# Where a softmax is divided by its sum: the weights, or the attention's output

## Chip, cores, metric

One of the eight cores of a Trainium2 chip. The time is the device time of one execution in microseconds; the median of the runs counts. Engines: TensorE (PE, with its weight loads PEld), VectorE (DVE), ScalarE (ACT), GpSimd (POOL), SyncE (SP, which issues loads).

## The reference

Two transformer blocks over 512 tokens of width 1024, in fp32. The parts that matter are the attentions of the two mixers; each block has one mixer.

```python
# first block, dsa_attention: 8 query heads of 64, one shared key/value head,
# of the keys up to the query's position the best 128 are kept
logits = einsum('bqhd,bqkd->bqhk', qb, k_sel) * attn_scale
p = softmax(where(valid, logits, -inf), axis=-1)
out = einsum('bqhk,bqkd->bqhd', p, v_sel)

# second block, blocked_attention, twice: 8 heads with keys of 64+32 and values of 64,
# and 8 query heads of 64 over 2 key/value heads
s = einsum("bqhgd,bkhd->bhgqk", qblk, k)
pr = softmax(s, axis=-1)
out = einsum("bhgqk,bkhd->bqhd", pr, v)
```

The first block also has a cross-attention to 256 memory tokens (4 heads of 256). Around them stand the feed-forward layers, gates, projections and norms.

## The kernel before

Activations lie feature-major, 128 features on the partitions and 512 tokens along the row, in eight tiles. Every large product is made of three matmuls over operands split into a high and a low part (`mm3`); VectorE makes the low parts and ScalarE the high ones, also for each weight that a load brings.

An attention is a series of units. A unit of the first mixer is one block of 128 queries with four heads (`group`, L878), 4 blocks x 2 groups = 8 units, with 128, 256, 384 or 512 keys. The second mixer has 8 units of one head with four query blocks each (`head`, L1323), then 8 units of `group` with 512 keys. Each unit first makes four logits tiles with queries on the partitions in three `lg` banks of PSUM and calls `softmax` (L826) on each: maximum over the row and the bias from it on VectorE (L833 or L836, L838 or L840), exponential on ScalarE, which also writes the row's sum into `z` (L841), reciprocal of `z` (L842) and multiplication of the 128 x n weights by it (L850). The tables `F4` and `F6` in `K` send one multiplication in four of `head` and of the first mixer to GpSimd; the rest is VectorE's.

Then `pv` (L864) goes over the key tiles: `turned` (L852) transposes the four weight tiles on TensorE into one of the two `tt` banks (L858), splits them (L860 on ScalarE, L861 on VectorE), and two matmuls add high and low part into the one `o` bank (L872, L873). The value operand holds the high part in columns 0 to 63 and the low part in 64 to 127, so the output stands in two halves of 64 partitions, which have to be added: ScalarE copies the lower half to SBUF (L875), and VectorE adds the upper one into the result (L893 in `group`, four pieces of 64 x 128; L1337 in `head`, one of 64 x 512). In the output the queries run along the row, so a factor for each query is a row there, while the sums are a column.

`overlapped` (L896) writes the program so: the logits and softmax of unit u + 1, then a piece of other work (gates, keys, queries: projections that give TensorE something to do), then `pv` of unit u. The order that the engines get is not that of the program: a planner goes through all instructions with the program's order as priority, with durations of its own, and puts each on its engine when its operands and a free buffer are there by its reckoning. Buffers of one tag are a ring: a bank is given away again when its last reader is done. On the chip each engine follows its list in order.

`row` (L588) was there before, for the norms: it transposes a column, broadcast to 128 x 128, so that each partition of a PSUM tile holds it as a row. In cross-attention (`cross`, L1131) 16 calls of `softmax` divide the weights too.

Of the kernel before, what the change touches and what calls it, by code (L numbers as in the profile page):

```python
# [14 lines left out]
AF = mybir.ActivationFunctionType  # L15
OP = mybir.AluOpType
# [3 lines left out]
P = 128  # L20
D = 1024
KD = D // P
S = 512
NT = S // P
M = 256
# [30 lines left out]
A, B = slice(0, S // 2), slice(S // 2, S)  # L56
# [3 lines left out]
K = {'slots': [32, 8, 5],  # L60
 'F1': 0,
 'F2': 0,
 'F3': 1,
 'F4': 'PVVV',
 'F5': 'VVVV',
 'F6': 'VVPV',
 'ga0': 4,
 'gb0': 4,
# [110 lines left out]
class Net:  # L179
# [643 lines left out]
        mm(ps[:, :n], lhsT=q[:, qs], rhs=hh[:, :n], start=True, stop=False)  # L823
        mm(ps[:, :n], lhsT=q[:, qs], rhs=ll[:, :n], start=False, stop=True)

    def softmax(self, ps, scale, n, bias=None, pool="V"):  # L826

        nc = self.nc
        p = self.tmp((P, n))
        m, nb, z = (self.small(t, [P, 1], 8) for t in ("sm_m", "sm_b", "sm_z"))  # L830
        src = ps[:, :n]
        if bias is not None:
            nc.vector.tensor_tensor_reduce(out=p, in0=src, in1=bias, op0=OP.add, op1=OP.max, scale=1.0, scalar=NEG, accum_out=m)  # L833
            src = p
        else:
            nc.vector.tensor_reduce(out=m, in_=src, axis=AX.X, op=OP.max)  # L836
        if isinstance(scale, float):
            nc.vector.tensor_scalar(nb, m, -scale, None, op0=OP.mult)  # L838
        else:
            nc.vector.scalar_tensor_tensor(nb, m, -1.0, scale, op0=OP.mult, op1=OP.mult)  # L840
        nc.scalar.activation(p, src, AF.Exp, bias=nb, scale=scale, accum_out=z)  # L841
        nc.vector.reciprocal(z, z)  # L842
        self.scale(p, p, z, pool)
        return p

    def scale(self, out, src, z, pool="V"):
        if pool == "A":
            self.nc.scalar.activation(out, src, AF.Copy, scale=z)
            return
        (self.nc.gpsimd if pool == "P" else self.nc.vector).tensor_scalar(out, src, z, None, op0=OP.mult)  # L850

    def turned(self, ps_, j):  # L852

# [7 lines left out]
        nc.vector.tensor_tensor(lo, ps[:, :n], hi.bitcast(F32), op=OP.subtract)  # L861
        return hi, lo

    def pv(self, ps_, v):  # L864


        mm = self.nc.tensor.matmul
        o = self.bank("o")
        last = len(v) - 1
        for j, vj in enumerate(v):  # L870
            hi, lo = self.turned(ps_, j)
            mm(o, lhsT=vj, rhs=hi, start=j == 0, stop=False)  # L872
            mm(o, lhsT=vj, rhs=lo, start=False, stop=j == last)  # L873
        low = self.slot("u", (64, S))
        self.nc.scalar.copy(low, o[64:128])  # L875
        return o, low

    def group(self, i, g, q, keys, v, ot, n, soft):  # L878

        nc = self.nc  # L880
        ps = []
        for j in range(4):
            hd = 4 * g + j
            l = self.bank("lg")

            self.logits(l, q[hd], hd % 2, i, keys, max(n, 2 * P))
            ps.append(soft(l, hd, j))
        yield
        o, low = self.pv(ps, v[: n // P])
        for e in range(2):  # L890
            for c in range(2):
                b = slice((2 * c + e) * P, (2 * c + e + 1) * P)
                nc.vector.tensor_tensor(  # L893
                    ot[2 * g + c][64 * e : 64 * e + 64, i * P : i * P + P], o[0:64, b], low[:, b], op=OP.add)

    def overlapped(self, units):  # L896

# [41 lines left out]
    def mix(self):  # L939
        self.phase = "mix"  # L940
        nc, h = self.nc, self.h
# [85 lines left out]
        def units():  # L1027
            for i in range(NT):
                for g in range(2):
                    yield self.group(i, g, qa, ka, v, ot, (i + 1) * P,  # L1030
                                     lambda l, hd, j: self.softmax(l, 0.125, (i + 1) * P, bias[i], pool=K["F6"][j])), [lambda: next(more_b, None)]

        self.overlapped(units())
        for _ in more_b:
# [96 lines left out]
    def cross(self):  # L1131
        self.phase = "cross"
        nc, h = self.nc, self.h
        xs, r, step = self.enter("xattn_pre_g")
        keys, vals, work = self.memory()
        self.begin([], step, work)
        self.attending = True
        os_ = []

        def head(hd):  # L1140
            q = [self.split(self.project("xattn_w_q", 2 * hd + d, xs, r), self.pair()) for d in range(2)]
            ps = []
            for i in range(NT):
                l = self.bank("lg")
                for d in range(2):
                    qq = tuple(part[:, i * P : i * P + P] for part in q[d])
                    self.mm3(l[:, :M], qq, keys[2 * hd + d], d == 0, d == 1)
                ps.append(self.softmax(l, 0.0625, M))
            yield
            pt = [self.turned(ps, j) for j in range(2)]  # L1150
            for d in range(2):
                o = self.bank("o" if d else "lg")
                c = (hd % 2) * M + d * P
                for j in range(2):
                    vv = tuple(part[:, c : c + P] for part in vals[hd // 2, j])
                    self.mm3(o, vv, pt[j], j == 0, j == 1)
                os_.append(self.split(o, self.pair()))

        self.overlapped((head(hd), ()) for hd in range(4))
        self.attending = False  # L1160
        f = [self.big(dt=F32) for _ in range(KD)]
        self.down("xattn_w_o", f, 0, os_, False, K["late:cross"])
        self.leave(f, "xattn_post_g")

    def mix2(self):
# [155 lines left out]
            next(more_a)  # L1321

        def head(hd, q, keys):  # L1323
            ps = []
            for i in range(NT):
                l = self.bank("lg")
                tok = slice(i * P, i * P + P)
                self.mm3(l, (q[0][:, tok], q[1][:, tok]), keys, True, True)
                ps.append(self.softmax(l, sca[:, i : i + 1], S, pool=K["F4"][i]))
            yield  # L1330
            o, low = self.pv(ps, [t[:, hd % 4, :] for t in va[hd // 4]])
            own = slice(64 * (hd % 2), 64 * (hd % 2) + 64)
            if K["oa"][hd] == "P":
                nc.scalar.copy(oa[hd // 2][own], o[0:64])
                nc.gpsimd.tensor_tensor(oa[hd // 2][own], oa[hd // 2][own], low, op=OP.add)
            else:
                nc.vector.tensor_tensor(oa[hd // 2][own], o[0:64], low, op=OP.add)  # L1337

        ob = []

        def units():
            for hd in range(H):
                yield head(hd, *ready[hd]), work.pop(0)
                if hd % 2 and hd + 1 < H:
                    ready.extend(prepare(hd + 1))
            for _ in more_a:
                pass
            ob.extend(self.big(dt=F32) for _ in range(4))
            for g in range(2):
                for i in range(NT):  # L1350
                    yield self.group(i, g, qb, kbs[g], vbs[g], ob, S,
                                     lambda l, hd, j: self.softmax(l, scb[hd // 2][:, 2 * i + hd % 2 : 2 * i + hd % 2 + 1], S, pool=K["F5"][j])), work.pop(0)

        self.overlapped(units())
        for _ in more_b:
# [278 lines left out]
```

## Time and profile before

| | us |
|---|---|
| median of 3 runs | 2098.67 |
| lowest, highest | 2090.48, 2103.62 |
| profiled execution, own time | 2091.38 |
| its span, first to last instruction | 2089.6 |

On a busy line a share belongs to the whole span; a window gives busy time in one stretch, so idle time of an engine there is the stretch less its figure. Matmuls overlap, and their ends are modelled, so a busy TensorE is not one at its peak. In the waits the engine left of the arrow stood idle until the one on the right was done.

### The profile page before, as it was taken

The page shows a single profiled execution, that of the slowest core. Times are in us where ns is not written, and L with a number is a line of the kernel's source. Part 1 is how long each engine was busy: PE and PEld are TensorE (multiplying, and loading weights), DVE is VectorE, ACT ScalarE, POOL GpSimd, SP SyncE. Part 2 cuts the span into 40 slices and gives each one's busy share as a digit, 9 for nine tenths or more (in the row PEclk, how much of TensorE's full clock was granted, in tenths as well). Part 3 has the DMA queues.
Part 4 walks back from the last instruction along what each step waited for, and adds up shares of the span by engine and source line. Part 5 has one row for each costly group of instructions (what it writes and reads, how often), then busy time and mean ns, then how long its engine had stood idle before and what let it go on. Part 6 is the DMA issues. An engine that isn't in the chain of part 4 may idle for free. (4 is left out here: it accounts for less than half of the span.)

```text
span 2089.6 us, 32337 instructions
## 1 busy us (share of the span) xinstructions
PE 2011.4 (96%) x12428; PEld 1766.1 (85%) x12428; DVE 1544.4 (74%) x2956; ACT 1101.7 (53%) x2052; POOL 254.4 (12%) x239
## 2 busy tenths in 40 slices
PE   8999999899999999999999998998999999999997
PEld 7899998778778888998999998776778888988997
DVE  7977786799775585587777869588987678666755
ACT  5644454673573454554445445467864436444752
POOL 2000002313331310040000003213100000000001
PEclk9999999899999999999999999999999999999999
DMA  5233333212222233221333342211112313323331
GB/s 163 91 112 97 106 107 122 71 61 91 91 71 95 77 120 103 93 70 51 113 110 102 106 141 72 66 41 51 41 41 81 114 31 122 99 89 104 112 101 41
DMA packets 66010, 186.43 MB, mean 89 GB/s; under 512 B 6976, under 2 KB 14144, under 8 KB 65856
## 3 DMA queue, kind: packets, MB, share of 16 engines
q1 hardware_dynamic: 63376, 180.97, 26.8%
q10 hardware_dynamic: 2448, 3.41, 0.5%
q8 instruction: 97, 1.59, 0.3%
q14 instruction: 57, 0.47, 0.1%
q0 software_dynamic: 32, 0.00, 0.0%
HBM read 182.25 MB, written 2.10 MB: 88 GB/s over the span
## 5 line engine op out<-in xcount | busy, mean ns | idle before, releaser
L290 PE MATMUL mm<-x,w 128*128 128x512 f32 (+1 forms) x2064 | 473.8, 379 | 0.0
L290 PE MATMUL mm<-b,w 128*128 128x256 f32 (+1 forms) x2625 | 448.6, 322 | 2.0 <-ACT b L510 1.8
L290 PEld LDWEIGHTS mm<-x,w 128*128 128x128 f32 x2064 | 364.0, 188 | 74.9 <-DVE v L1274 0.7
L290 PEld LDWEIGHTS mm<-b,w 128*128 128x128 f32 x2625 | 375.2, 188 | 48.9 <-ACT b L510 4.2
L252 ACT CAST w<-r 128x1024 fp32r<-128x1024 f32 (+2 forms) x256 | 229.8, 898 | 277.8 <-PE mm L290 118.0
L290 PE MATMUL lg<-x,w 128*128 128x256 f32 (+1 forms) x2460 | 348.6, 295 | 6.8 <-DVE t L1385 4.7
L253 DVE TENSOR_TENSOR w<-r,w 128x1024 fp32r<-128x1024 f32 (+2 forms) x254 | 267.8, 1055 | 116.3 <-ACT w L252 111.3
L290 PE MATMUL lg<-b,w 128*128 128x256 f32 (+1 forms) x1929 | 352.9, 334 | 0.0
L290 PEld LDWEIGHTS lg<-x,w 128*128 128x128 f32 x2460 | 315.9, 188 | 27.9 <-DVE t L1385 6.4
L290 PEld LDWEIGHTS lg<-b,w 128*128 128x128 f32 x1929 | 294.5, 188 | 42.1
L457 ACT CAST w<-r 128x1024 fp32r<-128x1024 f32 x147 | 154.6, 1053 | 138.1 <-PE lg L290 81.3
L458 DVE TENSOR_TENSOR w<-r,w 128x1024 fp32r<-128x1024 f32 x147 | 178.7, 1221 | 19.9 <-ACT w L457 19.4
L290 PE MATMUL mm<-x,u 128*128 128x256 f32 x756 | 108.1, 287 | 15.6 <-ACT x L513 7.1
L510 ACT CAST b<-t 128x512 fp32r<-128x512 f32 (+1 forms) x113 | 60.8, 539 | 112.5 <-DVE t L745 34.3
L290 PEld LDWEIGHTS mm<-x,u 128*128 128x128 f32 x756 | 96.9, 193 | 18.7 <-ACT x L513 7.5
L569 POOL TENSOR_TENSOR sh<-sh,sh 128x256 f32<-128x256 f32 x45 | 37.5, 834 | 502.8 <-ACT sh L563 499.9
L511 DVE TENSOR_TENSOR b<-t,b 128x512 fp32r<-128x512 f32 (+1 forms) x113 | 67.2, 596 | 26.3 <-ACT b L510 26.0
L569 POOL TENSOR_TENSOR sf<-sf,sf 128x256 f32<-128x256 f32 x28 | 23.3, 833 | 450.4 <-ACT sf L563 440.4
L563 ACT ACTIVATE sh<-h 128x256 f32<-128x256 f32 x128 | 49.9, 411 | 52.5 <-DVE h L630 22.7
L928 POOL TENSOR_TENSOR b<-b,rows 128x512 f32<-128x512 f32 x32 | 52.5, 1642 | 174.7 <-ACT b L926 174.7
L861 DVE TENSOR_TENSOR u<-tt,u 128x512 fp32r<-128x512 f32 x92 | 62.0, 684 | 9.9 <-ACT u L860 9.3
L290 PE MATMUL lg<-x,b 128*128 128x256 f32 x456 | 68.1, 291 | 0.0
(271 smaller groups left out, 2738.9 us busy)
## 6 DMA issues: line engine op xcount, KB each, us to landing
r<-in_ffn_w SPq DMA_DIRECT2D x86, 512.0 KB, 3.3
r<-in_w_in SPq DMA_DIRECT2D x64, 512.0 KB, 3.2
r<-in_ffn_w SPq DMA_DIRECT2D x68, 256.0 KB, 2.7
r<-in_w_up SPq DMA_DIRECT2D x32, 512.0 KB, 3.2
r<-in_w_down SPq DMA_DIRECT2D x32, 384.0 KB, 3.4
r<-in_ffn_w SPq DMA_DIRECT2D x16, 384.0 KB, 3.3
r<-in_w_out SPq DMA_DIRECT2D x8, 512.0 KB, 3.2
r<-in_xattn_w_k SPq DMA_DIRECT2D x8, 512.0 KB, 3.2
```

The source lines that it names most:

```text
L252: nc.scalar.copy(hi, raw)
L253: self.second.tensor_tensor(lo, raw, hi.bitcast(F32), op=OP.subtract)
L290: self.nc.tensor.matmul(ps, lhsT=lhsT, rhs=rhs, start=start, stop=stop, skip_group_check=on)
L457: nc.scalar.copy(hi, raw)
L458: nc.vector.tensor_tensor(lo, raw, hi.bitcast(F32), op=OP.subtract)
L510: nc.scalar.copy(hi, src)
L511: nc.vector.tensor_tensor(lo, src, hi.bitcast(F32), op=OP.subtract)
L563: nc.scalar.activation(t, x, AF.Square)
L569: eng.tensor_tensor(ts[0], ts[0], t, op=OP.add)
L861: nc.vector.tensor_tensor(lo, ps[:, :n], hi.bitcast(F32), op=OP.subtract)
L928: nc.gpsimd.tensor_tensor(t[:, tok], t[:, tok], r[:, tok], op=OP.mult)
```

## The change

`softmax` stops after the exponential and leaves its weights undivided; the sums of a unit's four tiles go into the four columns of one tile. `pv`, after the copy of the lower half, takes one reciprocal of the 128 x 4 sums, turns its four columns into a row of 512 factors with `row` (four transposes into a `tt` bank), and adds the two halves of the output into `low`. `group` and `head` then multiply `low` by the row of factors, in the pieces in which they added before. All these multiplications are VectorE's, and the tables that sent some work to GpSimd have no reader any more. Cross-attention keeps reciprocal and multiplication, written at its call.

```diff
--- before.py
+++ after.py
@@ -823,11 +823,12 @@
         mm(ps[:, :n], lhsT=q[:, qs], rhs=hh[:, :n], start=True, stop=False)
         mm(ps[:, :n], lhsT=q[:, qs], rhs=ll[:, :n], start=False, stop=True)
-    def softmax(self, ps, scale, n, bias=None, pool="V"):
+    def softmax(self, ps, scale, n, z, bias=None):
+
         nc = self.nc
         p = self.tmp((P, n))
-        m, nb, z = (self.small(t, [P, 1], 8) for t in ("sm_m", "sm_b", "sm_z"))
+        m, nb = (self.small(t, [P, 1], 8) for t in ("sm_m", "sm_b"))
         src = ps[:, :n]
         if bias is not None:
             nc.vector.tensor_tensor_reduce(out=p, in0=src, in1=bias, op0=OP.add, op1=OP.max, scale=1.0, scalar=NEG, accum_out=m)
@@ -839,15 +840,10 @@
         else:
             nc.vector.scalar_tensor_tensor(nb, m, -1.0, scale, op0=OP.mult, op1=OP.mult)
         nc.scalar.activation(p, src, AF.Exp, bias=nb, scale=scale, accum_out=z)
-        nc.vector.reciprocal(z, z)
-        self.scale(p, p, z, pool)
         return p
-    def scale(self, out, src, z, pool="V"):
-        if pool == "A":
-            self.nc.scalar.activation(out, src, AF.Copy, scale=z)
-            return
-        (self.nc.gpsimd if pool == "P" else self.nc.vector).tensor_scalar(out, src, z, None, op0=OP.mult)
+    def sums_of(self, count):
+        return self.small("sm_z", [P, count], 8)
     def turned(self, ps_, j):
@@ -861,7 +857,7 @@
         nc.vector.tensor_tensor(lo, ps[:, :n], hi.bitcast(F32), op=OP.subtract)
         return hi, lo
-    def pv(self, ps_, v):
+    def pv(self, ps_, z, v):
         mm = self.nc.tensor.matmul
@@ -873,25 +869,28 @@
             mm(o, lhsT=vj, rhs=lo, start=False, stop=j == last)
         low = self.slot("u", (64, S))
         self.nc.scalar.copy(low, o[64:128])
-        return o, low
+        self.nc.vector.reciprocal(z, z)
+        rz = self.row(z)
+        self.nc.vector.tensor_tensor(low, o[0:64], low, op=OP.add)
+        return low, rz[0:64]
     def group(self, i, g, q, keys, v, ot, n, soft):
         nc = self.nc
-        ps = []
+        ps, z = [], self.sums_of(4)
         for j in range(4):
             hd = 4 * g + j
             l = self.bank("lg")
             self.logits(l, q[hd], hd % 2, i, keys, max(n, 2 * P))
-            ps.append(soft(l, hd, j))
+            ps.append(soft(l, hd, z[:, j : j + 1]))
         yield
-        o, low = self.pv(ps, v[: n // P])
+        o, rz = self.pv(ps, z, v[: n // P])
         for e in range(2):
             for c in range(2):
                 b = slice((2 * c + e) * P, (2 * c + e + 1) * P)
                 nc.vector.tensor_tensor(
-                    ot[2 * g + c][64 * e : 64 * e + 64, i * P : i * P + P], o[0:64, b], low[:, b], op=OP.add)
+                    ot[2 * g + c][64 * e : 64 * e + 64, i * P : i * P + P], o[:, b], rz[:, b], op=OP.mult)
     def overlapped(self, units):
@@ -1028,7 +1027,7 @@
             for i in range(NT):
                 for g in range(2):
                     yield self.group(i, g, qa, ka, v, ot, (i + 1) * P,
-                                     lambda l, hd, j: self.softmax(l, 0.125, (i + 1) * P, bias[i], pool=K["F6"][j])), [lambda: next(more_b, None)]
+                                     lambda l, hd, z: self.softmax(l, 0.125, (i + 1) * P, z, bias[i])), [lambda: next(more_b, None)]
         self.overlapped(units())
         for _ in more_b:
@@ -1145,7 +1144,11 @@
                 for d in range(2):
                     qq = tuple(part[:, i * P : i * P + P] for part in q[d])
                     self.mm3(l[:, :M], qq, keys[2 * hd + d], d == 0, d == 1)
-                ps.append(self.softmax(l, 0.0625, M))
+                z = self.sums_of(1)
+                p = self.softmax(l, 0.0625, M, z)
+                nc.vector.reciprocal(z, z)
+                nc.vector.tensor_scalar(p, p, z, None, op0=OP.mult)
+                ps.append(p)
             yield
             pt = [self.turned(ps, j) for j in range(2)]
             for d in range(2):
@@ -1321,20 +1324,16 @@
             next(more_a)
         def head(hd, q, keys):
-            ps = []
+            ps, z = [], self.sums_of(NT)
             for i in range(NT):
                 l = self.bank("lg")
                 tok = slice(i * P, i * P + P)
                 self.mm3(l, (q[0][:, tok], q[1][:, tok]), keys, True, True)
-                ps.append(self.softmax(l, sca[:, i : i + 1], S, pool=K["F4"][i]))
+                ps.append(self.softmax(l, sca[:, i : i + 1], S, z[:, i : i + 1]))
             yield
-            o, low = self.pv(ps, [t[:, hd % 4, :] for t in va[hd // 4]])
+            o, rz = self.pv(ps, z, [t[:, hd % 4, :] for t in va[hd // 4]])
             own = slice(64 * (hd % 2), 64 * (hd % 2) + 64)
-            if K["oa"][hd] == "P":
-                nc.scalar.copy(oa[hd // 2][own], o[0:64])
-                nc.gpsimd.tensor_tensor(oa[hd // 2][own], oa[hd // 2][own], low, op=OP.add)
-            else:
-                nc.vector.tensor_tensor(oa[hd // 2][own], o[0:64], low, op=OP.add)
+            nc.vector.tensor_tensor(oa[hd // 2][own], o, rz, op=OP.mult)
         ob = []
@@ -1349,7 +1348,7 @@
             for g in range(2):
                 for i in range(NT):
                     yield self.group(i, g, qb, kbs[g], vbs[g], ob, S,
-                                     lambda l, hd, j: self.softmax(l, scb[hd // 2][:, 2 * i + hd % 2 : 2 * i + hd % 2 + 1], S, pool=K["F5"][j])), work.pop(0)
+                                     lambda l, hd, z: self.softmax(l, scb[hd // 2][:, 2 * i + hd % 2 : 2 * i + hd % 2 + 1], S, z)), work.pop(0)
         self.overlapped(units())
         for _ in more_b:
```

## Rows read from the trace of the kernel before

**Rows 1.** The page, busy times of the engines, and the granted clock in 40 slices:

```profile
PE 2011.4 (96%) x12428; PEld 1766.1 (85%) x12428; DVE 1544.4 (74%) x2956; ACT 1101.7 (53%) x2052; POOL 254.4 (12%) x239
...
PEclk9999999899999999999999999999999999999999
```

**Rows 2.** Windows over the three attentions of the mixers, with their columns:

```profile
core 0: us, PE busy (x) PEld busy (x) DVE busy (x) ACT busy (x) POOL busy (x), PEclk, DMA share, GB/s
546.00:606.00 60.00, 58.90 (x298) 47.59 (x297) 49.27 (x186) 44.89 (x106) 20.54 (x15) 1.00 0.16 53
1355.00:1470.00 115.00, 102.35 (x481) 78.19 (x480) 95.06 (x230) 84.33 (x166) 26.98 (x17) 0.97 0.13 45
1470.00:1580.00 110.00, 105.29 (x512) 80.26 (x511) 95.75 (x252) 80.16 (x154) 13.55 (x10) 1.00 0.13 44
```

**Rows 3.** Windows of 15 us inside the second mixer:

```profile
1400.00:1415.00 15.00, 13.61 (x69) 10.62 (x70) 14.60 (x34) 11.46 (x24) 1.57 (x1) 1.00 0.16 50
1415.00:1430.00 15.00, 10.54 (x52) 8.70 (x50) 10.25 (x28) 8.16 (x15) 2.01 (x2) 0.89 0.18 57
1430.00:1445.00 15.00, 11.62 (x50) 8.07 (x49) 12.49 (x26) 11.66 (x26) 7.14 (x5) 0.88 0.07 26
1445.00:1460.00 15.00, 15.00 (x75) 12.17 (x74) 14.38 (x35) 11.93 (x23) 3.89 (x2) 1.00 0.23 81
```

**Rows 4.** Chain, 1355-1470 and 1470-1580 by line; pieces (start, us, what) of 1355-1580:

```profile
by line: PE mm L290 27.8%; PE lg L290 14.8%; PE tt L858 6.6%; PE o L873 5.1%; DVE u L861 5.0%; PE o L872 4.1%; DVE t L850 3.8%; issue 3.4%; DVE sm_m L836 2.9%; DVE w L253 2.7%; ACT t L841 2.4%; DVE b L1255 2.3%; PE mm L1272 2.3%; DVE sm_b L
...
by line: PE mm L290 31.6%; PE o L872 8.6%; PE tt L858 8.6%; PE o L873 7.0%; PE lg L823 4.1%; issue 4.0%; PE lg L824 3.6%; ACT u L860 3.6%; POOL b L928 3.3%; DVE u L861 2.9%; DVE b L803 2.5%; ACT w L252 2.2%; DVE w L253 2.1%; DVE t L850 1.7%
...
1369.43 0.87 PE tt L858 x8
...
1414.34 5.61 PE mm L290 x24
```

**Rows 5.** Waits, 1355 to 1580 us: who <- for whom: us, times, longest:

```profile
ACT t L841 <- DVE sm_b L840: 12.5, 17, 1.6
PEld o L873 <- DVE u L861: 11.5, 14, 3.2
PEld o L872 <- ACT u L860: 10.1, 28, 1.5
...
PE mm L1293 <- DVE t L1290: 4.5, 1, 4.5
```

**Rows 6.** Windows of L850 alone (VectorE, GpSimd where any); line L842, ns min/median/max:

```profile
546.00:606.00 60.00, 10.78 (x24) 9.84 (x8) 1.00 0.16 53
1355.00:1470.00 115.00, 13.99 (x24) 13.66 (x8) 0.97 0.13 45
1470.00:1580.00 110.00, 16.36 (x32) 0.00 (x0) 1.00 0.13 44
...
L842 DVE RECIPROCAL sm_z<-sm_z x112: 136/156/166, 548.2 to 1567.1; 128x1 f32<-128x1 f32 x112
```

**Rows 7.** Lines by form: count, busy us, mean ns of one, idle before:

```profile
L893 DVE TENSOR_TENSOR b<-o,u 64x128 f32<-64x128 f32 x64 | 15.4, 278 | 5.2 <-ACT u L875 4.6
...
L875 ACT COPY u<-o 64x512 f32<-64x512 f32 x24 | 14.0, 584 | 14.1 <-PE o L873 13.6
...
L593 PE MATMUL tt<-ident,r 128*128 128x128 f32 x54 | 10.5, 281 | 5.5 <-DVE r L543 5.3
...
L1337 DVE TENSOR_TENSOR b<-o,u 64x512 f32<-64x512 f32 x8 | 5.5, 682 | 1.9 <-ACT u L875 1.6
```

**Rows 8.** Timeline, TensorE: last P·V matmul of a unit, next unit's transposes (first, last of 13):

```profile
576.88 0.48 PE L873 MATMUL o<-u,v 128*128 128x512 f32 x1
...
577.20 0.71 PE L858 MATMUL tt<-ident,t 128*128 128x128 f32 x5
...
1572.00 0.40 PE L873 MATMUL o<-u,v 128*128 128x512 f32 x1
1572.23 0.60 PE L858 MATMUL tt<-ident,t 128*128 128x128 f32 x4
```

## The prediction, made before the changed kernel was run

> **What bounds the kernel now.** I read the page's busy times first, then windows over the stretches that the change touches, then the chain of work and the waits inside them. On the page TensorE is busy for 96% of the span at a granted clock of nine tenths or more in 39 of 40 slices, VectorE for 74% [rows 1]: what TensorE has to issue sets most of the time, and an edit elsewhere counts only where TensorE stands still for it. The three windows show how different the two mixers are [rows 2]. In the first mixer's attention (546 to 606 us) TensorE is busy 58.90 of 60 us: hardly anything to win. In the second mixer's (1355 to 1470 its first attention, 1470 to 1580 its second) it is busy 102.35 of 115 and 105.29 of 110 us, so 12.65 + 4.71 = 17.4 us stand idle, while VectorE is busy 95.06 + 95.75 = 190.8 us of 225, or 85%. In slices of 15 us [rows 3] VectorE reaches 14.60 and 14.38 us: there it is nearly full. The slice at 1415 us is the loosest for TensorE, 10.54 us. The waits [rows 5] name the way in which VectorE holds TensorE up: a P·V matmul on the low halves (L873) waits 11.5 us in all for VectorE's subtraction at L861, and ScalarE's exponentials wait 12.5 us for VectorE's bias at L840, upon which the next logits wait for a free bank.
>
> **What is removed.** 24 units pass through `pv`: 8 in the first mixer, 16 in the second, each with four softmaxes. Each softmax loses a reciprocal of 128x1 (156 ns, [rows 6]) and a multiplication of its weights by it (L850). The 16 of those that stand on GpSimd go too; nothing waits for GpSimd's in the waits shown, so I cost them at nothing. On VectorE the multiplications took 10.78 us in the first mixer and 13.99 + 16.36 = 30.35 us in the second [rows 6]. Reciprocals: 32 x 0.156 = 5.0 and 64 x 0.156 = 10.0 us. Together 15.8 and 40.3 us of VectorE. Cross-attention (16 softmaxes) keeps both steps, only written elsewhere: no change.
>
> **What is added on VectorE.** For each unit one reciprocal of 128x4, for which the nearest row is the 128x1 one, 136 to 166 ns; I take 0.156 us. And one addition of the two 64x512 halves of the output, of the shape and operands (one in PSUM, one in SBUF) of L1337, 0.682 us [rows 7]. Sum 0.84 us a unit, so 6.7 us in the first mixer and 13.4 us in the second. The last step was an addition and becomes a multiplication of the same count and size (L1337, or four of 278 ns at L893 [rows 7]); one operand stays in PSUM, now the row of factors in place of the output, so the price stays. Net, VectorE is freed of 9.1 us in the first mixer and 26.9 us in the second, 14% of its 190.8.
>
> **What is added on TensorE.** Four transposes of 128x128 a unit, 96 in all: `row` turns each column of reciprocals into a row, as at L593, whose matmul lasts as long as that of the other transposes. One in a train costs 0.87 / 8 = 0.109 us [rows 4], so 32 x 0.109 = 3.5 us in the first mixer, 64 x 0.109 = 7.0 us in the second, 10.5 in all. Bounds: nothing, where each falls into idle time; 96 x 0.281 us [rows 7] = 27 us, if each stood alone. I take the train price, since the four are issued together, and charge it by the share in which TensorE is busy: all of 3.5 in the first mixer, 207.6 / 225 = 92% of 7.0 in the second, 6.5.
>
> [...]
>
> **Waits that move.** Before, weights were ready for their transposes after exponential, reciprocal and multiplication; now after the exponential. Nothing is shown waiting for L850, since a unit's `pv` follows the next unit's logits, so this shortening itself is worth nothing. New is a wait of TensorE for the reciprocal, with the following matmuls behind it; its input, the sums, is a unit old, and the planner can put it wherever VectorE is free, so I cost it at nothing, bounded by the 0.156 us of a reciprocal a unit, 3.7 us. The row of factors sits in one of the two `tt` banks until the last multiplication. After the last P·V matmul come the copy (0.584), the new addition (0.682) and four multiplications (4 x 0.278): 2.4 us. At 13 of 22 changes from unit to unit within a mixer the next unit's transposes start within 1 us of that matmul (first and last in [rows 8]); their second batch then needs this bank. But the `o` bank already holds the next unit's first P·V back until L893 has read it, and it is let go earlier now (one addition, 0.682 us, in place of 1.1 us of small ones). I charge nothing and keep 13 x 2.4 = 31 us as the bound. No DMA and no SP queue is touched.
>
> **What the freed VectorE is worth.** In the first mixer VectorE was busy 49.27 of 60 us and TensorE full: I take 0.5 us of the 1.1 idle. In the second the chain of work runs through L850 for 3.8% of 115 us and 1.7% of 110 us [rows 4]: 4.4 + 1.9 = 6.3 us that go directly, the lower bound. The upper one is all of TensorE's idle time, 17.4 us. The unknown lies between, since a shorter queue in front of L861 and L840 also shortens the 11.5 and 12.5 us of waits; part of the idle time has another cause (4.5 us are one wait for the keys' factors at L1293 [rows 5]). I take the middle, 12 us.
>
> **The sum.** +3.5 + 6.5 - 0.5 - 12 = -2.5 us against the profiled execution, whose own time is 2091.4 us (span 2089.6). That one lies 7.3 us below the median of the runs shown, 2098.7, within their spread of 2090.5 to 2103.6. Carried to the median: 2098.7 - 2.5 = 2096 us, the same within what can be told apart.
>
> **Rivals.**
> (a) The bank. A row of factors that keeps a `tt` bank stops the next unit's second batch of transposes, and TensorE stands. For it: the 13 close changes [rows 8], only two banks. Against it: TensorE has other matmuls ready in most units, up to 24 in a row (5.61 us, [rows 4]). Price: 31 us if all 13 are paid in full, so 2098.7 + 31 + 10 - 12.5 = 2127 us; it makes the kernel slower by over 1% from some 10 full waits on, 24 us.
> (b) VectorE sets the second mixer's pace. Then its freed 26.9 us come off up to where TensorE is full. For it: slices with 14 of 15 us busy [rows 3]. Against it: in those same slices TensorE is at 13.61 and 15.00 of 15 us. Time: all 17.4 us of idle time go and the transposes there fall into it, the first mixer pays 3: 2098.7 - 14.4 = 2084 us.
> (c) The change doesn't do what it says: VectorE's time falls and nothing follows, since TensorE's waits end on ScalarE (10.1 us for L860 [rows 5]). Only the transposes are left: 2098.7 + 10 = 2109 us.
> (d) The clock falls. Were the whole second mixer at 0.885 like the slices at 1415 to 1445 [rows 3], 225 x 0.115 = 26 us less 3.5 already paid would be lost: 2096 + 22 = 2118 us. Against it: 1.00 in the stretch with the most transposes. [...]
>
> **How the numbers follow.** The forecast has 0.54, (c) 0.20, (b) 0.16, (a) 0.07, (d) 0.03. What a measurement of this kernel can tell from no change is about 1%, 21 us. The range runs from (b) with some spread of the runs, 2082, to past (c) with one or two bank waits, 2114; it leaves out most of (a) and (d), and 0.05 for a planner that, with other instructions to place, orders both mixers anew for better or worse. The likeliest case's own range is 2088 to 2105. Faster by over 1% would need more than all of TensorE's idle time in these stretches, 0.06; slower by over 1% has (a), part of (d) and the planner, 0.09; 0.85 for within 1%.
>
> **What would show it.** Right: VectorE's busy time falls by some 36 us and GpSimd's by some 23 (9.84 + 13.66 [rows 6]); TensorE has 96 transposes more at L593's line; TensorE's idle time at 1355 to 1580 us falls to below 10 us; the first mixer's attention ends 3 us later. Wrong: transposes waiting for multiplications at the end of `group` or `head` would be (a); a second mixer shorter by over 12 us (b); unchanged waits for L861 with less busy VectorE (c); a granted clock below 1.00 in new places (d).

## The result, and the profile after

The changed kernel takes 2116.3 us (median of 6 runs, 2109.3 to 2121.1), the kernel before 2099.2 us beside it: ratio 1.0086, with an interval of 1.0067 to 1.0105, or 18 us more. That is within the 1% that I called no change, but it is a loss, 20 us above the forecast of 2096 and 2 us past the range. Its profiled execution takes 2114.07 us, span 2112.2.

The page's busy times and granted clock after:

```profile
PE 2031.5 (96%) x12524; PEld 1780.7 (84%) x12524; DVE 1522.9 (72%) x2828; ACT 1103.1 (52%) x2052; POOL 232.5 (11%) x223
...
PEclk9999999899999999999999999999999999999999
```

Against [rows 1], TensorE has the 96 transposes more (12524 against 12428) and is busy 20.1 us longer; VectorE is busy 21.5 us less, GpSimd 21.9 us less. The clock's row is the same.

The stretches of the attentions after: the first mixer's, then the second mixer's two parts (columns as in [rows 2]):

```profile
core 0: us, PE busy (x) PEld busy (x) DVE busy (x) ACT busy (x) POOL busy (x), PEclk, DMA share, GB/s
546.00:623.00 77.00, 74.09 (x378) 59.21 (x378) 48.12 (x155) 52.22 (x119) 17.49 (x12) 0.99 0.18 59
1365.00:1480.00 115.00, 103.57 (x503) 79.25 (x502) 86.85 (x189) 82.43 (x165) 12.16 (x9) 0.97 0.15 50
1480.00:1600.00 120.00, 110.96 (x550) 83.73 (x548) 88.07 (x202) 80.40 (x153) 13.80 (x9) 1.00 0.11 36
```

From the table load before its first exponential to its last P·V matmul the second mixer takes 235 us where it took 224, the first 77 where it took 70. VectorE is busy 174.9 us in the second mixer in place of 190.8 [rows 2]. And TensorE, which the freed VectorE was to serve better, stands idle 11.4 + 9.0 = 20.5 us there, not 17.4. Over the whole span its idle time is 80.7 us (2112.2 - 2031.5) against 78.2 (2089.6 - 2011.4).

The waits of the second mixer after, largest first (who waits for whom, us, times, longest):

```profile
PEld o L868 <- ACT u L856: 17.1, 36, 1.5
...
ACT b L1055 <- POOL b L927: 13.0, 10, 2.4
PEld o L869 <- DVE u L857: 9.0, 12, 1.4
...
ACT t L842 <- DVE sm_b L841: 7.4, 8, 2.2
```

L856, L857 and L841 are the cast, the subtraction and the bias of before (L860, L861, L840). The two waits that end on VectorE, which I had counted as winnable, did shrink, from 11.5 and 12.5 us [rows 5] to 9.0 and 7.4. The wait for ScalarE's cast grew from 10.1 to 17.1. What was gained at one place came back at another.

None of these rows is idle time of the matmuls: PEld is the queue of the weight loads, ACT is ScalarE. The matmuls' own waits (PE) in the second mixer are, before,

```profile
PE o L873 <- DVE u L861: 6.1, 9, 2.6
...
PE o L872 <- ACT u L860: 2.8, 3, 1.2
PE lg L290 <- ACT t L841: 2.4, 2, 1.3
```

with the 4.5 us for the keys' factors (L1293) that [rows 5] has, and after,

```profile
PE o L868 <- ACT u L856: 5.7, 9, 1.2
PE o L869 <- DVE u L857: 5.0, 6, 1.0
```

with 4.4 us for the keys. They show the same shift: a little less idle time that ends on VectorE's subtraction, more that ends on ScalarE's cast.

### The profile page after: what moved, and what is told of

It is laid out like the page before. It is cut to its first block, busy times and chain, and to the rows that moved or that the text cites. A ratio compares the mean times of both kernels' runs of the same rounds, so it can differ in the third digit from the quotient of the medians.

```text
span 2112.2 us, 32393 instructions
## 1 busy us (share of the span) xinstructions
PE 2031.5 (96%) x12524; PEld 1780.7 (84%) x12524; DVE 1522.9 (72%) x2828; ACT 1103.1 (52%) x2052; POOL 232.5 (11%) x223
## 3 DMA queue, kind: packets, MB, share of 16 engines
q8 instruction: 98, 1.61, 0.3%
## 5 line engine op out<-in xcount | busy, mean ns | idle before, releaser
L458 DVE TENSOR_TENSOR w<-r,w 128x1024 fp32r<-128x1024 f32 x147 | 178.6, 1220 | 21.5 <-ACT w L457 21.4
L857 DVE TENSOR_TENSOR u<-tt,u 128x512 fp32r<-128x512 f32 x92 | 62.6, 687 | 22.6 <-ACT u L856 22.0
```

Source lines behind the costliest of these rows:

```text
L458: nc.vector.tensor_tensor(lo, raw, hi.bitcast(F32), op=OP.subtract)
```

## The experiments

All ratios are to the kernel before, run beside each on the same chip; us over before are the ratio's excess times 2098. Code is shortened to what matters.

**1 to 4. Which part costs?** Rows that nobody reads, rows that hold their bank, the removal alone, and rows in another bank. Free rows first:

```diff
-        return o, low
+        return o, low, self.row(z)
...
+        nc.vector.tensor_tensor(junk, t[:, i * P : i * P + 1], t[:, i * P + 1 : i * P + 2], op=OP.mult)
```

and for the rows that are held, in place of the last line,

```diff
+        nc.vector.tensor_tensor(junk, t[:, i * P : i * P + 1], rz[64:128, 0:1], op=OP.mult)
```

both on the kernel before, with a unit's sums in one tile of four columns as after, `t` the unit's output. On the changed kernel, the removal alone and the other bank:

```diff
-        self.nc.vector.reciprocal(z, z)
-        rz = self.row(z)
-        self.nc.vector.tensor_tensor(low, o[0:64], low, op=OP.add)
-        return low, rz[0:64]
+        return o[0:64], low
...
-                    ot[2 * g + c][64 * e : 64 * e + 64, i * P : i * P + P], o[:, b], rz[:, b], op=OP.mult)
+                    ot[2 * g + c][64 * e : 64 * e + 64, i * P : i * P + P], o[:, b], rz[:, b], op=OP.add)
...
-        rz = self.row(z)
+        rz = self.row(z, lambda: self.bank("lg"))
```

> The kernel before (weights scaled as there, output computed in full) with four transposes more in each of the 24 units: the unit's four columns of reciprocals are turned to rows in a tt bank that nothing reads, so that the bank is free at once; one VectorE multiplication of 64x1 a unit, on SBUF alone, is added as a counterpart to the next kernel. Theory 'price' (the transposes cost their issue time, 24 x 0.39 us as read from the changed kernel): 9 to 11 us over the kernel before, ratio 1.0045 to 1.0055. Theory 'order' (any new instruction lets the planner order both mixers worse): 15 us or more. Theory 'bank': as 'price', since the bank is not held.

> As the kernel with rows that nothing reads, but the one 64x1 multiplication at the end of each unit reads the row of reciprocals, so that its tt bank is held until the unit's last addition; the output is that of the kernel before. Theory 'bank' (the held bank makes the new waits): 7 us or more over the kernel with free rows, 16 to 20 us over the kernel before, with waits of P-V for the ScalarE cast up as in the changed kernel. Theory 'price': within 3 us of the kernel with free rows.

> The changed kernel without what it adds: the sums are neither inverted, nor turned, nor multiplied on, and the last step of a unit is the addition of before; the attention's output of both mixers is left undivided. What is left is VectorE relieved of 96 reciprocals and 80 multiplications and GpSimd of 16. My prediction's step: 12.5 us less than before (ratio 0.994). Theory 'relief is worth nothing': within 3 us of before. Theory 'order': slower than before by 4 us or more although nothing is added.

> The changed kernel with one edit: the row of factors lies in a bank of the three of the logits (lg), not in one of the two of the transposes (tt). Theory 'bank': the new waits go, 7 us or more below the changed kernel, ratio to before 1.005 or less. Theories 'price' and 'order': within 3 us of the changed kernel, ratio 1.007 to 1.010. If the lg ring itself becomes short, logits wait for L892 or L1336 and it is slower than the changed kernel.

Free rows: 1.0111 (1.0088 to 1.0135), 23 us over. Held rows: 1.0136 (1.0111 to 1.0162), 28 us; the 5 us between them are within the intervals. Removal alone: 1.0025 (1.0012 to 1.0038), 5 us over before. Rows in lg: 1.0101 (1.0081 to 1.0121), 21 us.

The last and the second give no sign of the bank: with the rows out of `tt` the kernel is no faster than the changed one, and holding it costs nothing that stands clear of the noise. The third is the finding of the study. With everything removed and nothing added, the kernel is not 12.5 us faster but slower. Its page, its second mixer from 1362 to 1590 us (a line of the windows, columns as above) and the waits of that stretch:

```profile
PE 2026.5 (96%) x12428; PEld 1778.5 (85%) x12428; DVE 1505.9 (72%) x2780; ACT 1102.3 (52%) x2052; POOL 230.3 (11%) x223
```

```profile
1362.00:1590.00 228.00, 207.84 (x981) 157.79 (x980) 162.21 (x360) 161.41 (x316) 25.35 (x18) 0.96 0.12 41
```

```profile
PEld o L868 <- ACT u L856: 15.9, 34, 2.4
...
PEld o L869 <- DVE u L857: 9.1, 13, 1.2
...
PE o L868 <- ACT u L856: 6.6, 7, 2.2
PE o L868 <- DVE b L1333: 4.3, 1, 4.3
PE o L869 <- DVE u L857: 4.2, 6, 0.8
```

VectorE is 38.5 us less busy over the span and 28.6 us less in the second mixer, where it now works 162 of 228 us. TensorE's idle time there is 228.0 - 207.8 = 20.2 us. The matmuls' waits for VectorE's subtraction fell from 6.1 to 4.2 us, those for ScalarE's cast rose from 2.8 to 6.6, and a wait of 4.3 us for the addition that ends a unit (L1333) stands where the keys' 4.5 were.

**5 to 8. The additions one by one.** No rows; rows made twice; the 64x1 product alone; the copy of the low half on VectorE:

```diff
-        rz = self.row(z)
-        return low, rz[0:64]
+        return low, low                   # no rows
...
+        self.row(z)
         rz = self.row(z)                  # rows twice
...
-        self.nc.scalar.copy(low, o[64:128])
+        self.nc.vector.tensor_copy(low, o[64:128])
```

> The changed kernel without its 96 transposes: the reciprocals are taken, but not turned to rows, and the last multiplication reads the undivided output twice instead of a row, so the attention's output is not that of the reference. VectorE keeps all of its new work. The kernel with the removal alone ran 4 us over before. Theory 'issue price' (the transposes cost the 9.3 us that the changed kernel's trace shows them to take of TensorE's queue): 9 us below the changed kernel, ratio to before 1.004 to 1.005. Theory 'double price' (they cost twice that, since TensorE's other work waits behind them): at most 4 us over before, ratio 1.002 or less. Theory 'VectorE's additions cost': within 4 us of the changed kernel.

> The changed kernel with each unit's row made twice, the first of them read by nothing: 96 transposes more, output as before. Theory 'issue price': 9 us over the changed kernel, 27 over before, ratio 1.013. Theory 'double price': 18 us over the changed kernel, ratio 1.017.

> The kernel before with the one 64x1 multiplication a unit of the kernel with free rows, and no transposes: what the counterpart and a new order by the planner cost by themselves. Theory 'issue price' needs this kernel some 10 us over before, so that the rows themselves cost the 9 to 11 that they issue. Theory 'double price': within 3 us of before, so that the rows cost some 20.

> The changed kernel with the copy of the low halves' sum (64x512, once a unit) on VectorE instead of ScalarE: VectorE's relief is spent on ScalarE, 24 x 0.58 = 14 us. Theory 'ScalarE sets the waits' (P-V waits for ScalarE's cast): 5 us or more below the changed kernel. Theory 'neither engine': within 3 us of the changed kernel.

No rows: 1.0034 (1.0023 to 1.0045), 7 us over before, so the changed kernel's rows are worth 0.0052, 11 us. Rows twice: 1.0146 (1.0127 to 1.0164), so the second set costs 0.0060, 12.5 us. The price by issue time, 9 to 10 us, agrees with both; the double price asked for at most 1.002 without rows and for 1.017 with two sets, and both lie outside the intervals. The product alone: 1.0016 (1.0001 to 1.0032), 3 us, so on the kernel before the same 96 transposes cost some 20. That part of the first run I can't place. The low copy on VectorE: 1.0094 (1.0066 to 1.0122), no different from the changed kernel, though ScalarE was relieved of some 12 us (busy 1090.7 against 1103.1): a lighter ScalarE by itself does not help either. Nor did VectorE's load hurt: it is 15.2 us busier than in the changed kernel (1538.1 against 1522.9), with copies that stand in the mixers.

The changed kernel on the transposes: its timeline after a P·V matmul in the second mixer, and TensorE's busy time at L593 there (windows, 1365 to 1600 us; PE busy, PEld busy, granted clock, DMA share, GB/s):

```profile
1479.43 0.47 PE L869 MATMUL o<-u,b 128*128 128x512 f32 x1
1479.74 0.60 PE L593 MATMUL tt<-ident,sm_z 128*128 128x128 f32 x4
1480.09 1.41 PE L290 MATMUL mm<-x,w 128*128 128x512 f32 x5
```

```profile
1365.00:1600.00 235.00, 10.83 (x64) 8.00 (x64) 0.99 0.13 43
```

Four transposes take 1480.09 - 1479.74 = 0.35 us of the queue, 0.088 us each, a little under the 0.109 us that was costed.

**9 to 11. VectorE to be loaded, and a link of the chain to be cut.**

```diff
+        for _ in range(2):                # loaded: end of pv, on the kernel before
+            nc.vector.tensor_reduce(out=junk, in_=self.h[0], op=OP.max)
...
-        nc.vector.tensor_tensor(lo, ps[:, :n], hi, op=OP.subtract)
+        nc.vector.tensor_tensor(lo, ps[:, :n], self.h[0][:, :n], op=OP.subtract)   # cut
```

> The kernel before with VectorE loaded more instead of less: in each of the 24 units two reductions of 128x512 whose results nothing reads (the nearest row, the maximum of the logits at L836, takes 0.68 us: 48 x 0.68 = 33 us, 22 of them in the second mixer, where VectorE was busy for 191 of 225 us). Output as before. Theory 'VectorE sets the second mixer's pace': 15 us or more over before. Theory 'chain' (TensorE's idle pieces are the length of the chain from transposes over cast and subtraction to P-V, with VectorE free when the cast ends): within 5 us of before.

> The kernel before with the subtraction at L861 reading an unrelated 128x512 tile in place of the high halves: same operation, size and count on VectorE, but it no longer waits for ScalarE's cast. The low halves of the weights are wrong by that, and so is the attention's output. Theory 'chain': the idle pieces that ended on the subtraction shrink by the cast's 0.6 us each, some 10 of them in the second mixer: 4 to 6 us less than before. Theory 'VectorE's queue' (the subtraction waits behind other VectorE work): within 2 us of before.

> Both at once: the changed kernel without reciprocals, rows and the multiplication (the output undivided, as in the kernel with the removal alone), and the subtraction reading an unrelated tile instead of the high halves. Theory 'chain': as far below the kernel with the removal alone as the cut brings on the kernel before, 4 to 6 us; the removal is worth nothing on top. Theory 'VectorE's queue': 8 to 12 us below before, since now nothing is left in front of the subtraction.

With 48 reductions more the kernel is 1.0022 (1.0010 to 1.0033), 4.6 us, slower. But the load did not land where it was meant to. The reductions depend on nothing in their unit, and in the list that VectorE got all of them end before the second mixer starts and none stands in the first mixer's attention either:

```profile
L877 DVE TENSOR_REDUCE junk<-h x48: 661/676/682, 403.7 to 1351.9; 128x1 f32<-128x512 f32 x48
```

So this kernel says nothing on a fuller VectorE in the mixers. The cut gives 1.0009 (0.9999 to 1.0018), removal and cut together 1.0032 (1.0017 to 1.0047). Here too the edit did not do what it was for. The subtraction reads another tile, but it still waits for the cast; the row before the change, then with the cut:

```profile
DVE u L861 <- ACT u L860: 6.3, 10, 1.1
...
DVE u L861 <- ACT u L860: 7.4, 11, 1.3
```

In both kernels with the cut each of the 92 subtractions starts after the cast of its tile has ended. What keeps the wait there is not shown. So these runs can't test my second theory, that TensorE waits out the chain from cast over subtraction to P·V. The trace of the kernel before speaks against it, and for the other one, that the subtraction waits in VectorE's queue. At the longest of the nine waits of the matmuls for L861, 2.6 us up to 1432.89:

```profile
1424.83 0.59 ACT L860 CAST u<-tt 128x512 fp32r<-128x512 f32 x1
...
1431.09 1.14 DVE L840 SCALAR_TENSOR_TENSOR sm_b<-sm_m,sca 128x1 f32<-128x1 f32 x1
1432.15 0.68 DVE L861 TENSOR_TENSOR u<-tt,u 128x512 fp32r<-128x512 f32 x1
```

The cast of this tile ends at 1425.42, and VectorE, last at work on a bias, starts the subtraction 6.73 us later. So it is with all nine: the cast had ended 0.34 to 6.73 us before, and VectorE was at other work.

What these kernels do show is how well the idle time of the second mixer repeats. With the cut TensorE's 12,428 matmuls stand in the order of before, one for one, and with the reductions those of the second mixer do; the idle time there is 225.0 - 207.55 = 17.5 (1357 to 1582 us, the line below) and 17.1 us, beside 17.4:

```profile
1357.00:1582.00 225.00, 207.55 (x984) 157.96 (x984) 190.79 (x479) 162.89 (x316) 39.03 (x26) 0.97 0.13 44
```

**12 to 14. The relief with all instructions kept, and new orders alone.** The multiplications of the weights cut to two columns; the second part of the second attention's keys moved one work item later, before or behind the values:

```diff
-        self.scale(p, p, z, pool)
+        self.scale(p[:, 0:2], p[:, 0:2], z, pool)
...
-'work': ['a', 'a', 'a', 'b', 'vK', 'V', '0', ...
+'work': ['a', 'a', 'a', 'b', 'vK', 'LV', '0', ...   # L: second_keys from `full` on; or 'VL'
```

> The kernel before with its 96 multiplications of the weights (80 on VectorE, 16 on GpSimd) cut to two columns each: the weights stay unscaled but for those columns, so the attention's output is not the reference's. No instruction and no dependency is gone, and VectorE is relieved of some 35 us. Theory 'relief is worth nothing': within 4 us of before. Theory 'the planner's new order takes it back': 5 to 12 us less than before.

> The kernel before with the second part of the second attention's keys (the factors spread, turned at L1293 and multiplied on) moved from the work item of the fifth unit to that of the sixth, ahead of the values. Nothing is added or removed. If the 4.5 us of TensorE's idle time at L1293 are that step waiting for its own factors with no other work behind it in the queue, they go: 3 to 5 us less than before. If not, within 2 us.

> As the kernel with the keys' second part one work item later, but behind the values in that item. Same expectations: 3 to 5 us less than before if the idle time at L1293 is that step's own wait, within 2 us if not.

Short scaling: 1.0072 (1.0050 to 1.0095), 15 us slower than before, the relief's second failure. Part of it is the clock: over its runs the granted clock averaged 0.984, over those of the kernel before beside it 0.987, by estimate some 6 us of 2098. Its second mixer:

```profile
1355.00:1583.00 228.00, 206.49 (x970) 156.20 (x969) 173.77 (x477) 160.59 (x314) 29.21 (x26) 0.96 0.13 44
```

The two kernels with the keys moved add and remove nothing: 1.0023 (1.0009 to 1.0037) and 1.0050 (1.0031 to 1.0069), 5 and 10 us slower. The second mixer of the first of them:

```profile
1357.00:1585.00 228.00, 207.27 (x983) 156.40 (x982) 188.32 (x479) 162.98 (x316) 39.17 (x26) 0.98 0.13 43
```

A new order by the planner, with one step's place changed, moves this kernel by that much, and the idle time there is 20.7 us, as with the removal, though VectorE has all its work. The matmuls' wait of 4.5 us for the keys is gone in both, but nothing was won by it: other waits took its place.

**15 to 18. ScalarE behind GpSimd.** In the kernel before, two pieces of some 1.15 us near the end of the second mixer (at 1525 and 1538 us) look like this (ScalarE, GpSimd, TensorE in the timeline):

```profile
1525.22 0.63 ACT L1056 ACTIVATE b<-b 128x512 f32<-128x512 f32 x1 [1.47 <-POOL b L928]
1525.76 0.57 ACT L860 CAST u<-tt 128x512 fp32r<-128x512 f32 x1
...
1523.34 1.85 POOL L928 TENSOR_TENSOR b<-b,rows 128x512 f32<-128x512 f32 x1 [11.07 <-ACT b L926]
...
1526.38 0.50 PE L872 MATMUL o<-u,v 128*128 128x512 f32 x1 [1.15 <-ACT u L860]
```

TensorE's wait is put down to the cast. But the cast stands in ScalarE's queue behind a gate's Tanh, and that waits 1.47 us for GpSimd. VectorE has no part in it.

```diff
-                if len(late) > 1:         # Tanh one gate later
+                if len(late) > 2:
...
-        t, job = self.projection(w, n + i, xs, r, self.big, True)
+        t, job = self.projection(w, n + i, xs, r, self.big, r is None)   # gates on VectorE
```

> The kernel before with each gate's Tanh issued two gates after its projection instead of one. Nothing is added or removed. Theory 'ScalarE blocked by GpSimd' (in the second mixer ScalarE waits 10.1 us in 8 times for the gates' multiplication, with the casts that TensorE needs queued behind): the three pieces of 1.15 us at the end of the second attention and more go, 3 to 8 us less than before. Theory 'any new order costs': 3 us or more above before.

> The kernel before with the gates' multiplication on VectorE, straight from PSUM (0.68 us, as the nearest VectorE operation of 128x512 on a bank), in place of ScalarE's copy and GpSimd's multiplication. Theory 'ScalarE blocked by GpSimd': 3 to 8 us less than before, unless VectorE, loaded by 10 x 0.68 us more in the second mixer, takes its place. Theory 'any new order costs': 3 us or more above before.

> The changed kernel with the gates' multiplication on VectorE in the same way: VectorE's freed time is spent on what ScalarE waits for. Theory 'ScalarE blocked by GpSimd': 5 us or more below the changed kernel (its ScalarE waits 13.0 us in 10 times there). Theory 'any new order costs': within 4 us of the changed kernel.

> The changed kernel with each gate's Tanh issued two gates after its projection. Theory 'ScalarE blocked by GpSimd': 4 us or more below the changed kernel. Theory 'any new order costs': within 4 us of the changed kernel.

Tanh later, on the kernel before: 1.0006 (0.9993 to 1.0019); on the changed one 1.0089 (1.0074 to 1.0104), beside the changed kernel's 1.0086. These two test neither theory: by their traces every engine's instructions stand in the order of before and of the changed kernel, one for one, so the Tanh came no later; in the first of them ScalarE's wait for GpSimd stayed, 10.1 us in 8 times. Gates on VectorE, on the kernel before: 0.9989 (0.9978 to 0.9999), 2.3 us faster, the one kernel of the study below the kernel before. Its second mixer in two parts:

```profile
1356.00:1468.00 112.00, 102.21 (x477) 78.64 (x476) 96.09 (x229) 79.55 (x158) 21.48 (x14) 0.95 0.14 48
1468.00:1579.00 111.00, 108.91 (x535) 83.64 (x534) 101.40 (x266) 81.19 (x155) 4.34 (x3) 1.00 0.13 43
```

TensorE's idle time is 9.8 + 2.1 = 11.9 us, 5.5 less, the two pieces are gone, and VectorE is busier than in any other kernel, 197.5 of 223 us. ScalarE and GpSimd have less to do here and the order is new, so the gain can't be put down to one of them. On the changed kernel the same edit gives 1.0090 (1.0072 to 1.0109), no difference; its idle time there is 242.0 - 223.9 = 18.1 us, 2.4 below the changed kernel's.

The runs side by side, from the windows over each one's second mixer (us):

| kernel | VectorE busy | TensorE idle | stretch | over before, whole kernel |
|---|---|---|---|---|
| removal alone | 162.2 | 20.2 | 228 | +5 |
| short scaling | 173.8 | 21.5 | 228 | +15 |
| changed | 174.9 | 20.5 | 235 | +18 |
| before | 190.8 | 17.4 | 225 | 0 |
| keys moved, ahead of the values | 188.3 | 20.7 | 228 | +5 |
| cut (the wait stayed), same order | 190.8 | 17.5 | 225 | +2 |
| reductions (outside the mixers) | 191.7 | 17.1 | 225 | +5 |
| gates on VectorE | 197.5 | 11.9 | 223 | -2 |

Read down the second and third columns: less work on VectorE did not bring less idle time on TensorE in any of these kernels, and with VectorE busiest it is least. That does not show that VectorE never holds TensorE up: in the kernel before, 6.1 us of the matmuls' idle time end on a subtraction that stood behind other VectorE work. It shows that the relief, in the order that the planner made of it, was not turned into TensorE's time.

## Why the prediction was wrong

**What bounds the kernel** held: TensorE is busy for 96% of the span after, too. What did not hold was that its idle time in the second mixer is VectorE's to give back.

**What the freed VectorE is worth** is the step that failed: I took 12 us in the second mixer and 0.5 in the first, and the removal alone measured 5 us (2.5 to 8) the other way. That is 17.7 us of a miss of 20.5. Three readings went wrong in it. The lower bound of 6.3 us took a step's share of the chain of work [rows 4] for time that goes with the step; take it out, and the next latest input decides. The upper bound of 17.4 us took all idle time as VectorE's: it named the 4.5 us for the keys' factors and left them in, and of the rest 2.8 us end on ScalarE's cast and 2.4 on its exponentials. And the 11.5 us of waits for L861 [rows 5] are those of the weight loads (PEld); the matmuls themselves wait 6.1 us for it. That much is VectorE's, and it is half of the 12 that were taken. What the removal showed in its place: of these 6.1 us 1.9 went, the waits for the cast grew by 3.8, and TensorE's idle time in the second mixer rose from 17.4 to 20.2 us.

**What is removed and added on VectorE** was too high as busy time: 38.5 us less for the removal, where 56.1 were counted, and 1524.2 - 1505.9 = 18.3 us for the additions (no rows against removal alone), where 20.1 were. Records of neighbouring instructions overlap, two reciprocals taking 0.22 us (at 1394.12 us in the kernel before) where 2 x 0.156 were counted: summed over all of VectorE's instructions the durations fall by 52.1 us with the removal, but 13.6 us of that had lain under others (and other instructions grew by some 4). It did not matter, since the freed time was not turned into anything.

**What is added on TensorE** held: 10 us charged, 11 and 12.5 measured by taking the rows away and by doubling them. On the kernel before the same transposes cost some 20 us, and that stays open, so the price holds for the changed kernel alone. The first mixer, 3 us longer by the forecast, took 7 more: TensorE is busy 74.09 us there in place of 68.80 (546 to 616 us before) and idle 2.9 in place of 1.2.

**Waits costed at nothing** (the reciprocal, the bank) held as far as the runs can tell: rows in another bank won nothing, and no rows against the removal alone, which has neither reciprocal nor addition, is 2 us with overlapping intervals. So the 18 us part into 5 for the removal, 2 for VectorE's additions and 11 for the rows; they add up by construction, as steps on one way from the kernel before to the changed one.

**The clock**, rival (d): the granted clock averaged 0.987 over the runs of the changed kernel and 0.986 to 0.987 over those of the kernel before beside the experiments, and it is 1.00 from 1480 to 1600 us, where nine units have their rows. That added transposes lower the granted clock no run shows; with twice the rows it averaged 0.9885. The slices of 0.89 and 0.88 in [rows 3] hold short stretches of a lower clock: over windows of 3 us it is 0.50 from 1427 to 1430 us, 1.00 from 1430.5 to 1433.5 and 0.50 from 1434 to 1437; the 3.5 us that (d) counts as paid are what these two slices lose by estimate, 15 x 0.11 + 15 x 0.12. The clock does blur the profiles, though: the profiled execution of the kernel before had 0.990, that of the removal 0.984, by estimate some 13 us of 2100, and with the same 12428 matmuls TensorE is busy 15.1 us longer in the second (2026.5 against 2011.4) while its idle time over the whole span is 77.3 us against 78.2. So the removal's 5 us rest on the medians of its runs, whose clocks differ by under 0.001.

**The rivals**: (a) and (b) fell with the runs above. (c) came nearest: VectorE's time falls and nothing follows, only the transposes are left, 2109 us. Its sign, unchanged waits for L861, fits in part: the matmuls' fell from 6.1 to 5.0 us, while those for the cast grew from 2.8 to 5.7. But ScalarE relieved of the low copies gained nothing, and (c) lacked the 7 us that removal and additions cost besides. The range ended 2 us short; I gave a new order by the planner 0.05 and left it out. Two kernels with a new order and nothing added or removed moved by 5 and 10 us, so it belonged inside. That the change stayed within 1%, as said, is no credit to the mechanism.

**What stays open** is how the removal comes to cost 5 us and the short scaling 15, some 6 of them clock. Both were ordered anew, and a new order alone has moved the time by 5 and 10 us and TensorE's idle time by as much as the removal. That the order takes back what the relief brings is argued, not shown: the removal in the order of before was not tried. Nor did any run load VectorE in the mixers of the kernel before with nothing else changed, or free the subtraction from its wait for the cast.

## What to carry to other kernels

Before a busy engine's relief is given a worth, go through the idle pieces of the engine that bounds the kernel one by one, and ask of each what stood ahead of the late instruction in its own queue; a wait names the last arrival, not the cause, and a wait of the weight loads is not idle time of the matmuls (for L861 here 11.5 us of the one, 6.1 of the other). Look in the trace whether an experiment's edit did what it was for: here added work was moved out of the stretch, a cut left the wait in place, and a later step came no later. Where a planner orders the instructions, price a new order too: here an edit that adds and removes nothing was worth up to 10 us, as much as most terms of the sum. Here work added to the bounding engine was paid in full, and work taken from another was not won.

## What the runs showed of the hardware

The multiplication of the weights (L850, VectorE) lasts longer beside some of GpSimd's instructions. Its durations in the second attention of the kernel before (min/median/max), and the longest one beside GpSimd's instruction of that moment:

```profile
L850 DVE TENSOR_SCALAR t<-t,sm_z x32: 472/479/1510, 1473.8 to 1567.3; 128x512 f32<-128x512 f32 x32
...
1558.00 1.30 POOL L928 TENSOR_TENSOR b<-b,rows 128x512 f32<-128x512 f32 x1 [19.91 <-ACT b L926]
...
1558.07 1.51 DVE L850 TENSOR_SCALAR t<-t,sm_z 128x512 f32<-128x512 f32 x1
```

Its median is 0.48 us; the one beside L928 takes 1.51 us and ends 0.28 us after it. At 1394 us one that is recorded 0.04 us ahead of L928 takes 1.61 us and ends 0.28 us after it too. With two columns in place of 512 (short scaling) the median is 0.22 us; the one beside L928 takes 1.18 us and ends 0.02 us after it:

```profile
L850 DVE TENSOR_SCALAR t<-t,sm_z x33: 215/222/1177, 1470.6 to 1571.7; 128x2 f32<-128x2 f32 x33
...
1513.14 1.29 POOL L928 TENSOR_TENSOR b<-b,rows 128x512 f32<-128x512 f32 x1 [7.08 <-ACT b L926]
...
1513.27 1.18 DVE L850 TENSOR_SCALAR t<-t,sm_z 128x2 f32<-128x2 f32 x1
```

So part of what the page of the profile counts as L850's busy time is spent where GpSimd works beside it, by estimate 1.51 - 0.48 = 1.03 us in the first pair and 1.18 - 0.22 = 0.96 us in the second. What makes these longer the trace does not show. Not every overlap is like that: in the kernel before thirteen of the 96 multiplications on VectorE start while one of GpSimd's own (L850) runs; three of them last 0.75 to 0.83 us, the other ten no longer than 0.49 us.

In the trace of the kernel before, the instructions of an engine stand in the order of its list in the program: GpSimd's 239 and ScalarE's 1935 (the separate reads of sums left out) one for one, and VectorE's 2860 outside L993.
